# Sliding-window attention of a fused encoder layer: from half chunks to whole chunks

## The chip, the cores and the metric

The kernel runs on one core of one Trainium2 chip, as one launch. The metric is the time of that launch on the device in microseconds, as the median of several runs; lower is better.

## The reference, cut to what matters

The program computes one layer of a streaming encoder in float32: 1024 prompt tokens and 64 sample tokens, model width 1024. The part that the change touches is sliding-window attention (SWA). Tokens come in chunks of 64: 16 chunks of the prompt and one of the sample, 17 in all. A chunk's 64 queries look at 192 keys (its own chunk and the two before it; the first two chunks of the prompt have 64 and 128 keys). There are 16 query heads of width 64 in two groups, and each group shares one key and value head.

```python
s = einsum('bnqhgd,bnkhd->bnhgqk', q, k) * 64 ** -0.5 + bias
m = maximum(max(s, axis=-1), sink)
e = exp(s - m)
p = e / (sum(e, axis=-1) + exp(sink - m))
out = einsum('bnhgqk,bnkhd->bnqhgd', p, v)
```

While SWA runs, the kernel also computes two products that need nothing from it, to keep TensorE busy: the values of the cross-attention memory, and the first output projection of the retention branch:

```python
mv = rms_norm(mem, g_mem) @ w_mv
a = (rms_norm(ret_o) * silu(ret_g)) @ w_ret_out
```

## The kernel before, in words

**Stages.** The kernel first projects the inputs (`project_phase`), with the large products done by Strassen's scheme (`strassen`, lines 208 to 211). Then comes the stage of the change (`mix_phase`, which calls `swa`), and after it the merge of the branches, cross-attention and the feed-forward network. A float32 product is made of three matmuls on rounded parts: `mm3` (lines 152 to 154) multiplies high by high, high by low and low by high. So each operand is first split in two: ScalarE rounds it (line 125) and VectorE subtracts (line 126).

**One half of a chunk.** 64 queries times 2 heads fill 128 partitions, so a chunk's 16 heads are 8 units, and a half (`hf`) is 4 of them. `scores` multiplies queries by keys into PSUM (line 1188; these matmuls use 64 of the 128 rows of the array), VectorE adds the bias into the tile `t` (line 1195, or 1201 for the two short chunks) and finds the minimum of each row (line 1198 or 1203). `softmax` has ScalarE take four exponentials with their sums (line 1214), VectorE invert the sums (line 1216) and GpSimd scale (line 1217). `turn` transposes the weights on TensorE with an identity matrix (line 1242 for the first 128 keys, line 1248 for the last 64); ScalarE copies the first result to SBUF (line 1243, tile `pT`) and VectorE the second (line 1249, tile `rT`). Once per chunk, `values` transposes the new value columns (line 1149) and ScalarE copies them out (line 1153). `weigh` multiplies by the values (lines 1259 and 1264) for a whole chunk, and VectorE copies the result into `osb` (line 1271), which is stored every other chunk.

**The order.** The loop at line 1279 runs over 34 halves. In one step TensorE gets: `weigh` of the last chunk (every other step), `scores` of the half two steps ahead, `turn` of this half, and then a piece or two of the other products. `in_order` keeps TensorE's instructions in the order of the program; on the other engines a scheduler sets the order when the kernel is built, and each engine then works strictly through its list. `fill` hands out the pieces: 8 of the memory values before the first `turn`, 40 of the output projection over the 34 steps, and 8 more behind the last `weigh`. A piece is 12 matmuls for the projection (4 blocks of `mm3`), and 12 for the values (24 matmuls per block of 128 memory tokens).

**The other products.** `filler` makes the memory values of two heads: `us` are the split weights, line 1356 scales the result out of PSUM and frees its bank, and two stores follow on SyncE's queue. Then it multiplies by `w_ret_out`: units 0, 1 and 2 (each 128 output columns) are loaded and split together before the first product, the split of 1 and 2 behind the last of those scaled copies (line 1365); `m_major` then goes through the three units chunk of tokens by chunk of tokens. During the first eight pieces, `operands` also splits the retention output of the remaining tokens (tiles `ret`, lines 125 and 126), two per piece, 16 in all. Line 1377 multiplies a finished product by the gate.

**PSUM.** There are eight banks. Before `mix_phase`, the projections use three pairs of banks in turn (`psa`) and two single ones. `mix_phase` then takes, in this order, `pturn` (two banks, for line 1242 and line 1248), `pout` (a pair, for `weigh`), `pw` (a pair, for `scores`) and two single banks for the pieces. So `scores` stands on the third pair of `psa`.

Of the kernel before, what the change touches and what calls it, by code (L numbers as in the profile page):

```python
# [14 lines left out]
ALU = mybir.AluOpType  # L15
# [95 lines left out]
class Kernel:  # L111
# [999 lines left out]
    def swa(self, ctx, fill):  # L1111
        nc, tc, io = self.nc, self.tc, self.io
        if True:
# [27 lines left out]

            def values(los):
# [4 lines left out]
                pt = self.dense_psum()  # L1147
                for j, lo in enumerate(new):
                    self.last_mm = nc.tensor.transpose(pt[:n, j * P:(j + 1) * P], flat[5][:, 64 + lo:64 + lo + n], self.ident).ins
                at = vts[0][0]  # L1150
                for lo in new:
                    vtok[lo] = vts.pop(0)[1]
                nc.scalar.copy(at[:n, :len(new) * P], pt[:n, :len(new) * P])
# [3 lines left out]
            halves = [(c, hf) for c in range(17) for hf in range(2)]  # L1157
            live, outs, self.turn_copy = {}, {}, None
# [19 lines left out]

            def scores(c, hf):
                ks, j0, nk = keys(c)  # L1180
                if hf == 0 and c % 4 == 2 and c + 2 < 17:
# [3 lines left out]
                pss = pw.tile([P, 2, 512], F32, tag="s", name="pss")  # L1185
                for i in range(2):
                    for v in range(2):
                        self.last_mm = mm(pss[:, v, i * NKEY:i * NKEY + nk], qT[rows[v], 2 * hf + i, c % 4, :],  # L1188
                                          kT[rows[v], ks:ks + nk], start=True, stop=True).ins
                t = logits[hf]  # L1190
                ps = pss[:, :, :2 * NKEY].rearrange("p v (i n) -> p v i n", n=NKEY)
                bs = bias.rearrange("p (v h i) n -> p v h i n", v=2, h=2)[:, :, hf]
                nm = sw.tile([P, 2, 2], F32, tag="nm", name="nm")
                if nk == NKEY:
                    nc.vector.scalar_tensor_tensor(t[:, :, 1:wide_row - 1], pss[:, :, :2 * NKEY], -0.125,
                                                   bs.rearrange("p v i n -> p v (i n)"), ALU.mult, ALU.subtract)
                    both = t.rearrange("p v (i n) -> p v i n", i=2)
                    self.max_done = nc.vector.tensor_reduce(nm, both, AX.X, ALU.min).ins  # L1198
                else:
                    for i, x in enumerate(inner(t, nk)):  # L1200
                        nc.vector.scalar_tensor_tensor(x, ps[:, :, i, :nk], -0.125, bs[:, :, i, j0:], ALU.mult, ALU.subtract)
                    for i, x in enumerate(parts(t, nk)):
                        self.max_done = nc.vector.tensor_reduce(nm[:, :, i:i + 1], x.unsqueeze(2), AX.X, ALU.min).ins
                live[c, hf] = nm

            def softmax(c, hf):
# [17 lines left out]

            def turn(c, hf):
                ks, j0, nk = keys(c)
                wide = nk == NKEY
                if hf == 0:
                    values([ks + P, ks - 64, ks + 64, ks] if wide else [ks])
                    tail = [vtok[ks + P], vtok[ks - 64]] if wide else None  # L1230
                    live[c] = [vtok[ks + 64 * i if wide else ks] for i in range(2)], tail
                    tall = sw.tile([P, 4, 2, P], F32, tag="pT0", bufs=1, name="pT")
                    rest = sw.tile([P, 2, 2, P], F32, tag="pT1", bufs=1, name="rT") if wide else None
                    outs[c] = tall, rest
                tall, rest = outs[c]
                t = live.pop((c, hf))
                n = min(P, nk)
                pp = self.pt.tile([P, 512], F32, tag="pt0", name="pp")
                for j, (v, i) in enumerate(units):
                    a = 64 * i if wide else 0  # L1240
                    x = inner(t, nk)[i][:, v, a:a + n]
                    self.last_mm = nc.tensor.transpose(pp[:n, j * P:(j + 1) * P], x, self.ident).ins
                self.turn_copy = nc.scalar.copy(tall[:n, :, hf, :], pp[:n, :].rearrange("p (u q) -> p u q", u=4)).ins
                if wide:
                    pp = self.pt.tile([P, 512], F32, tag="pt1", name="pr")
                    for v in range(2):
                        x = t[:, v, 1 + P:1 + 2 * P]
                        self.last_mm = nc.tensor.transpose(pp[:, v * P:(v + 1) * P], x, self.ident).ins
                    nc.vector.tensor_copy(rest[:, :, hf, :], pp[:, :2 * P].rearrange("p (v q) -> p v q", v=2))

            def weigh(c):
# [9 lines left out]
                if rest is not None:  # L1261
                    for v in range(2):
                        for i in range(2):
                            self.last_mm = mm(po[rows[v], i, :2 * P], tail[i][rows[i], rows[v]], row(rest[rows[i], v]),
                                              start=False, stop=True).ins
                if c % 2 == 0:
                    outs["osb"] = sw.tile([P, KT, 2, 64], F32, tag="osb", bufs=2, name="osb")
                osb = outs["osb"]
                to = osb[:, :, c % 2, :].rearrange("p (h i e) q -> p h i e q", h=2, i=2)
                for i in range(2):  # L1270
                    nc.vector.tensor_copy(to[:, :, i], po[:, i, :2 * P].rearrange("p (h e q) -> p h e q", h=2, e=2))
                if c % 2 == 1 or c == 16:
# [4 lines left out]

            n = len(halves)
            for i in range(-2, n):
                if i > 0 and i % 2 == 0:  # L1280
                    self.in_order(lambda: weigh(i // 2 - 1))
                if i + 2 < n:
                    self.in_order(lambda: scores(*halves[i + 2]))
                if i >= 0:
                    self.in_order(lambda: turn(*halves[i]))
                if i + 2 < n:
                    softmax(*halves[i + 2])
                for pieces in next(fill):
                    self.in_order(lambda: next(pieces, None))
                if i == 8:  # L1290
                    with tc.issue_after(self.last_fetch):
                        keep()
            self.in_order(lambda: weigh(n // 2 - 1))
            for pieces in next(fill):
                self.in_order(lambda: next(pieces, None))

# [17 lines left out]
    def filler(self):  # L1314

        nc, tc, io = self.nc, self.tc, self.io
        if True:
# [24 lines left out]
            for h in range(2, H):  # L1342
# [5 lines left out]
                for t in range(2):  # L1348
# [6 lines left out]
                    o = ld()[:, :256]  # L1355
                    copied = nc.scalar.mul(o, ps[:, :256], self.mtok[:, t:t + 1]).ins
                    self.store(self.d_mv[h, :, t, :], o)
                    self.store(io["o_mv"][t * P:(t + 1) * P, h * 256:(h + 1) * 256], o)
                    yield

            def unit(m):
                raw = self.unit_raw(io["w_ret_out"][m], KT)
                if m not in (1, 2):
                    return self.unit_parts(raw, KT)
                with tc.issue_after(copied):
                    return self.unit_parts(raw, KT)

            units = [lambda m=m: unit(m) for m in range(KT)]
            for m, u, (c0, n) in self.m_major(units, CH, tail=1, lead=3):
                g = ld()  # L1370
# [651 lines left out]
```

## Time and profile before

| | us |
|---|---|
| median of three runs | 2193.73 |
| lowest and highest of them | 2190.91, 2196.80 |
| the profiled execution's own time | 2199.11 |
| its span, first to last instruction | 2197.1 |
| stage of the change: first `scores` | 804.2 |
| stage of the change: last `weigh` begins | 988.1 |

Times inside the profile count from the start of the span. PE is TensorE, DVE is VectorE, ACT is ScalarE, POOL is GpSimd and SP is SyncE. A row of the timeline gives start, duration, engine, line, operation, tiles, shape and count; in brackets stands how long the engine had been idle and what released it. PE is busy in 98% of the span, so what counts is the few microseconds in which it isn't, and the time that its own instructions take. A matmul's duration overlaps the next, so a cost on PE is read from starts. PEclk is the share of TensorE's clock that was granted.

### The profile page before, as it was taken

What the parts mean: (1) busy time and instruction counts of PE and PEld (TensorE: products, weight loads), DVE (VectorE), ACT (ScalarE), POOL (GpSimd) and SP (SyncE); (2) the same over time, 40 slices, a digit from 0 to 9 for tenths busy, and PEclk for the clock granted to TensorE, in tenths of its full rate; (3) what the DMA queues carried; (4) which work ended last, traced back from release to release, by engine and by line L of the source; (5) the groups of instructions that cost most, each with busy time, mean ns of one, the idle gap of its engine ahead of it and who ended that gap; (6) DMA issues with size and microseconds to landing.
All of it is one profiled execution on the core that took longest, in us unless ns stands there. A gap on an engine that the chain in (4) does not pass through costs nothing.

```text
span 2197.1 us, 41242 instructions
## 1 busy us (share of the span) xinstructions
PE 2154.6 (98%) x16388; PEld 2104.8 (96%) x16388; DVE 1574.0 (72%) x2569; ACT 875.0 (40%) x1826; POOL 616.9 (28%) x472
## 2 busy tenths in 40 slices
PE   9999999999999999999999999999999999999988
PEld 9999999999999997779999999999999999999987
DVE  7897878767678658766445555668877777779777
ACT  6434343436434356553233333333223222334333
POOL 0014535452264213220000000016655555431121
PEclk9999999999999999999999999999999999999999
DMA  4533434443454475427443121412432232466332
GB/s 172 185 113 113 145 115 158 131 133 108 142 181 158 146 252 185 133 73 226 131 156 114 40 69 55 139 60 95 142 122 96 93 130 80 147 245 221 112 106 92
DMA packets 160370, 291.84 MB, mean 133 GB/s; under 512 B 20946, under 2 KB 89490, under 8 KB 160050
## 3 DMA queue, kind: packets, MB, share of 16 engines
q1 hardware_dynamic: 150466, 263.41, 37.1%
q0 software_dynamic: 5104, 17.44, 2.2%
q10 hardware_dynamic: 4608, 8.36, 1.0%
q8 instruction: 129, 2.11, 0.4%
q14 instruction: 63, 0.52, 0.1%
HBM read 197.99 MB, written 91.95 MB: 132 GB/s over the span
## 4 chain that ended last, share of the span: by engine, by line
PE 79%; DVE 8%; DMA 6%; ACT 3%; issue 2%; POOL 2%; SPq 0%; DVEq 0%; ACTq 0%; POOLq 0%
PE pq L208 16%; PE pq L211 15%; PE pq L209 15%; PE pd L152 7%; PE pd L154 7%; PE pd L153 7%; DVE wq L126 1%; ACT e L1214 1%; DMA raw<-w_down 1%; PE pss L1188 1%; DVE stage L659 1%; DMA d_qkv<-stage 1%; DMA xg<-xT 1%; PE pk L894 1%; PE pout L1259 1%
## 5 line engine op out<-in xcount | busy, mean ns | idle before, releaser
L126 DVE TENSOR_TENSOR wq<-raw,wq 128x512 fp32r<-128x512 f32 (+1 forms) x498 | 454.5, 918 | 165.3 <-ACT wq L125 163.5
L125 ACT CAST wq<-raw 128x512 fp32r<-128x512 f32 (+1 forms) x498 | 299.5, 612 | 558.3 <-PE pq L211 186.4
L208 PE MATMUL pq<-T,wq 128*128 128x272 f32 x1800 | 496.1, 293 | 11.5 <-ACT wq L125 10.7
L209 PE MATMUL pq<-T,wq 128*128 128x272 f32 x1800 | 490.7, 289 | 0.0
L208 PE MATMUL pq<-B,wq 128*128 128x272 f32 x1550 | 424.3, 292 | 1.4 <-DVE stage L659 1.3
L209 PE MATMUL pq<-B,wq 128*128 128x272 f32 x1550 | 419.8, 288 | 0.0
L211 PE MATMUL pq<-T,wq 128*128 128x272 f32 x1800 | 374.2, 289 | 2.1 <-DVE wq L126 2.1
L186 POOL TENSOR_TENSOR raw<-raw 128x512 f32<-128x512 f32 (+1 forms) x49 | 69.1, 1411 | 1034.6 <-DVE rs_r L316 476.6
L208 PEld LDWEIGHTS pq<-T,wq 128*128 128x128 f32 x1800 | 341.4, 190 | 14.1 <-ACT wq L125 11.3
L209 PEld LDWEIGHTS pq<-T,wq 128*128 128x128 f32 x1800 | 344.8, 192 | 0.0
L211 PE MATMUL pq<-B,wq 128*128 128x272 f32 x1550 | 320.4, 287 | 0.0
L209 PEld LDWEIGHTS pq<-B,wq 128*128 128x128 f32 x1550 | 294.4, 190 | 0.0
L208 PEld LDWEIGHTS pq<-B,wq 128*128 128x128 f32 x1550 | 291.5, 188 | 2.7 <-ACT mraw L568 1.5
L211 PEld LDWEIGHTS pq<-T,wq 128*128 128x128 f32 x1800 | 281.2, 189 | 2.5 <-DVE wq L126 2.3
L211 PEld LDWEIGHTS pq<-B,wq 128*128 128x128 f32 x1550 | 240.2, 188 | 0.0
L277 DVE TENSOR_TENSOR u<-pq,u 128x544 f32<-128x544 f32 x174 | 124.6, 718 | 67.2 <-PE pq L211 66.9
L659 DVE TENSOR_TENSOR stage<-pq,u 128x544 f32<-128x544 f32 x108 | 77.4, 717 | 32.5 <-PE pq L211 22.8
L189 POOL TENSOR_TENSOR raw<-raw 128x512 f32<-128x512 f32 (+1 forms) x49 | 68.0, 1387 | 83.1 <-DVE wq L126 78.9
L1217 POOL TENSOR_TENSOR e<-e,den 128x768 f32<-128x768 f32 (+2 forms) x38 | 49.2, 1299 | 127.4 <-DVE den L1216 114.7
L1214 ACT ACTIVATE e<-t,nm 128x193 f32<-128x193 f32 (+2 forms) x136 | 59.1, 436 | 49.2 <-DVE nm L1198 48.3
L152 PE MATMUL pd<-xc,wq 128*128 128x256 f32 (+1 forms) x256 | 74.6, 291 | 0.2 <-DVE qf L1490 0.2
L192 POOL TENSOR_TENSOR raw<-raw 128x512 f32<-128x512 f32 (+1 forms) x49 | 70.4, 1437 | 15.3 <-DVE wq L126 12.2
(408 smaller groups left out, 4707.4 us busy)
## 6 DMA issues: line engine op xcount, KB each, us to landing
hl<-d_op SPq DMA_DIRECT2D x38, 544.0 KB, 5.2
d_op<-stage SPq DMA_DIRECT2D x44, 272.0 KB, 2.2
d_op<-ht SPq DMA_DIRECT2D x44, 272.0 KB, 3.3
raw<-w_gate SPq DMA_DIRECT2D x22, 512.0 KB, 3.5
raw<-w_up SPq DMA_DIRECT2D x22, 512.0 KB, 4.9
raw<-w_down SPq DMA_DIRECT2D x16, 512.0 KB, 3.8
d_gate<-stage ACTq DMA_DIRECT2D x28, 272.0 KB, 2.5
d_qkv<-stage SPq DMA_DIRECT2D x24, 272.0 KB, 2.3
```

Source lines behind the costliest of these rows:

```text
L125: self.last_cast = self.nc.scalar.copy(hi, src).ins
L126: self.last_low = self.nc.vector.tensor_tensor(out=lo, in0=src, in1=hi.bitcast(F32), op=ALU.subtract).ins
L152: mm(ps, wh, xh, start=start, stop=False)
L153: mm(ps, wh, xl, start=False, stop=False)
L154: self.last_mm = mm(ps, wl, xh, start=False, stop=stop).ins
L192: self.last_sum = tt(out=a12, in0=a12, in1=a11, op=sub).ins
L208: mm(ps[:, c, :HC], w[:, 0, ks], x[:, 0, cs], start=start, stop=False)
L209: mm(ps[:, c, :HC], w[:, 0, ks], x[:, 1, cs], start=False, stop=False)
L211: self.last_mm = mm(ps[:, c, :HC], w[:, 1, ks], x[:, 0, c * HC:(c + 1) * HC], start=False, stop=stop).ins
L277: add = lambda out, a, b: nc.vector.tensor_tensor(out=out, in0=a, in1=b, op=ALU.add)
L659: nc.vector.tensor_tensor(out=o, in0=ps, in1=sb, op=ALU.add)
L1214: self.exp_done = nc.scalar.activation(parts(e, nk)[i][:, v], parts(t, nk)[i][:, v], AF.Exp, scale=-1.0, bias=nm[:, v, i:i + 1], accum_out ...
```

## The change

1. **Whole chunks.** The loop runs over 17 chunks. TensorE's order in one step becomes: `weigh` of the last chunk, `scores` of both halves of the next chunk, a piece or two, `turn` of both halves of this chunk, a piece or two. `turn` copies both halves' first 128 keys at once (line 1244, 1024 elements per partition, where line 1243 had 512) and both rests at once (line 1252).
2. **Logits ahead of minima and copies.** VectorE adds the bias for both halves first, then finds the minima of both. The copies of the result into `osb` move from `weigh` into `gather` and stand behind the minima.
3. **Exponentials.** Those of the first half no longer stand behind the copy of the last `turn`; those of the second half still do.
4. **Values turned beside the rest.** `values` no longer takes a bank of the pieces: it writes into the second bank of the pair that `turn` uses for the rests, and its copy is line 1151.
5. **Pools swapped.** `pturn` is gone. `pw` comes first and has two pairs of banks, one per half, used by `scores` and then by `turn`; `pout` comes after it.
6. **First output weights.** Units 0 and 1 of `w_ret_out` are loaded together, unit 2 when it is first needed; units 1 and 2 are split at first use, behind the last copy of a `turn` on ScalarE.

```diff
-            self.pt, self.po, self.pw = (ctx.enter_context(self.tc.tile_pool(name=n, bufs=1, reuse_waits="tile", space=PSUM))
-                                         for n in ("pturn", "pout", "pw"))
+            self.pw, self.po = (ctx.enter_context(self.tc.tile_pool(name=n, bufs=1, reuse_waits="tile", space=PSUM))
+                                for n in ("pw", "pout"))
...
-                yield [pieces] * 4
-                yield [pieces] * 4
+                yield [pieces] * 8
...
+            area = lambda hf, name: pw.tile([P, 2, 512], F32, tag=f"s{hf}", name=name)
...
+                        self.max_done = nc.vector.scalar_tensor_tensor(
+                            t[:, :, 1:wide_row - 1], pss[:, :, :2 * NKEY], -0.125,
+                            bs.rearrange("p v i n -> p v (i n)"), ALU.mult, ALU.subtract).ins
+                        mins.append((nm, t.rearrange("p v (i n) -> p v i n", i=2)))
...
+                for nm, x in mins:
+                    with tc.issue_after(self.max_done):
+                        self.max_done = nc.vector.tensor_reduce(nm, x, AX.X, ALU.min).ins
...
-                with tc.issue_after(self.turn_copy) if self.turn_copy is not None else nullcontext():
+                with tc.issue_after(self.turn_copy) if hf and self.turn_copy is not None else nullcontext():
...
+                pr = area(1, "pr")
+                values([ks + P, ks - 64, ks + 64, ks] if wide else [ks], pr[:, 1, :])
...
+                self.turn_copy = nc.scalar.copy(tall[:n].rearrange("p u h q -> p h u q"),
+                                                pp[:n].rearrange("p h (u q) -> p h u q", u=4)).ins
...
+            for c in range(-1, 17):
+                if c > 0:
+                    self.in_order(lambda: weigh(c - 1))
+                if c < 16:
+                    self.in_order(lambda: scores(c + 1))
+                if c > 0:
+                    gather(c - 1)
+                if c < 16:
+                    softmax(c + 1, 0)
+                filled()
+                if c >= 0:
+                    self.in_order(lambda: turn(c))
+                if c < 16:
+                    softmax(c + 1, 1)
+                if c >= 0:
+                    filled()
...
+            raws = [self.unit_raw(io["w_ret_out"][m], KT) for m in range(2)]
+            done = {}
+
             def unit(m):
...
+                if m not in done:
+                    raw = raws[m] if m < 2 else self.unit_raw(io["w_ret_out"][m], KT)
+                    with tc.issue_after(self.turn_copy) if m in (1, 2) else nullcontext():
+                        done[m] = self.unit_parts(raw, KT)
+                return done[m]
```

The order in which instructions stand on an engine is fixed in the built program. Three places show what moved. The first is ScalarE around the memory values, before the change: `e` are the exponentials, `pd` the bank that line 1356 reads and frees, `wq` a split weight.

```order
L1214 ACT_TABLE_LOAD
L1214 ACTIVATE e_9694,den_9695<-t_9680,nm_9689 128x65 x4
L1356 ACTIVATE swin2_9521<-pd_9711,mtok_72 128x256
L125 CAST wq_9789<-raw_9641 128x512
L125 CAST wq_9792<-raw_9643 128x512
L125 CAST wq_9795<-raw_9643 128x512
L1356 ACTIVATE swin0_9424<-pd_9739,mtok_72 128x256
L1214 ACTIVATE e_9777,den_9778<-t_9681,nm_9772 128x65 x4
```

The same place after the change; line 1372 is what line 1356 was.

```order
L1215 ACT_TABLE_LOAD
L1215 ACTIVATE e_9701,den_9702<-t_9677,nm_9686 128x65 x4
L1215 ACTIVATE e_9842,den_9843<-t_9678,nm_9694 128x65 x4
L1372 ACTIVATE swin2_9521<-pd_9718,mtok_72 128x256
L125 CAST wq_9777<-raw_9641 128x512
L125 CAST wq_9780<-raw_9643 128x512
L125 CAST wq_9783<-raw_9643 128x512
L1372 ACTIVATE swin0_9424<-pd_9746,mtok_72 128x256
```

Both halves' exponentials now stand ahead of the first scaled copy and of three weight casts. The second place is ScalarE around chunk 0's `turn`, before the change: `pT` is the copy of line 1243, and `swin4<-pd` of line 1153 the copy of the turned values, both read by `weigh`.

```order
L125 CAST wq_9893<-raw_9891 128x512
L125 CAST wq_9896<-raw_9891 128x512
L1153 COPY swin4_9672<-pd_9864 128x128
L1243 COPY pT_9867<-pp_9868 64x4x128
L125 CAST wq_9901<-raw_9899 128x512
L125 CAST wq_9904<-raw_9899 128x512
L1214 ACTIVATE e_9874,den_9875<-t_9680,nm_9859 128x129 x4
L125 CAST ret0_9489<-swin6_9430 128x384
L125 CAST ret1_9492<-swin6_9430 128x384
L1243 COPY pT_9867<-pp_9937 64x4x128
```

After the change, the copy of the turned values is line 1151.

```order
L1215 ACTIVATE e_9871,den_9872<-t_9677,nm_9856 128x129 x4
L125 CAST ret0_9489<-swin6_9430 128x384
L125 CAST ret1_9492<-swin6_9430 128x384
L1244 COPY pT_9913<-pp_9914 64x2x4x128
L1215 ACTIVATE e_9924,den_9925<-t_9678,nm_9864 128x129 x4
L125 CAST ret4_9526<-swin6_9430 128x384
L125 CAST ret5_9529<-swin6_9430 128x384
L125 CAST wq_9986<-raw_9882 128x512
L125 CAST wq_9989<-raw_9882 128x512
L1151 COPY swin4_9669<-pr_9910 128x128
```

The copy of the turned values moved from ahead of everything to behind the second half's exponentials, two operand casts and the two casts of unit 1. The third place is VectorE in one later chunk, before the change.

```order
L1195 SCALAR_TENSOR_TENSOR t_9680<-pss_10402,swin2_9521 128x2x384
L1249 COPY rT_10414<-pr_10421 128x2x128
L1198 TENSOR_REDUCE nm_10407<-t_9680 128x4
L1377 TENSOR_TENSOR swin0_9424<-pd_10376,swin0_9424 128x384
L1195 SCALAR_TENSOR_TENSOR t_9681<-pss_10447,swin2_9521 128x2x384
L1216 RECIPROCAL den_10426<-den_10426 128x4
L1249 COPY rT_10414<-pr_10461 128x2x128
L1198 TENSOR_REDUCE nm_10452<-t_9681 128x4
```

And after the change.

```order
L1194 SCALAR_TENSOR_TENSOR t_9677<-pss_10378,swin2_9521 128x2x384
L1194 SCALAR_TENSOR_TENSOR t_9678<-pss_10385,swin2_9521 128x2x384
L1205 TENSOR_REDUCE nm_10383<-t_9677 128x4
L1205 TENSOR_REDUCE nm_10390<-t_9678 128x4
L1279 COPY osb_10394<-pout_10368 128x2x2x64 x2
L1396 TENSOR_TENSOR swin0_9424<-pd_10351,swin0_9424 128x384
L1217 RECIPROCAL den_10398<-den_10398 128x4
L1252 COPY rT_10423<-pr_10419 128x2x2x128
```

Both additions of the bias now come first, then both minima, then the copies; the copy of the rests is one instruction.

More of the change, by code (lines that the diff above doesn't have):

```diff
@@ L1140, in swa, with values @@
             vtok = {}
-            def values(los):
+            def values(los, pt):
                 new = [lo for lo in los if lo not in vtok]
@@ L1177, in keys, with scores @@
                 return kc + j0, j0, NKEY - j0
-            def scores(c, hf):
+            def scores(c):
                 ks, j0, nk = keys(c)
-                if hf == 0 and c % 4 == 2 and c + 2 < 17:
+                if c % 4 == 2 and c + 2 < 17:
                     with tc.issue_after(self.last_fetch):
@@ L1184, in scores @@
                 qT = qTs[c // 4 % 2]
[L1185 to L1203, printed above, removed]
@@ L1223, in softmax, with turn @@
                 live[c, hf] = e
-            def turn(c, hf):
+            def turn(c):
                 ks, j0, nk = keys(c)
                 wide = nk == NKEY
[L1228 to L1236, printed above, removed]
-                n = min(P, nk)
[L1238 to L1243, printed above, removed]
-                if wide:
[L1245 to L1249, printed above, removed]
@@ new lines, in turn @@
+                pr = area(1, "pr")
+                values([ks + P, ks - 64, ks + 64, ks] if wide else [ks], pr[:, 1, :])
+                tail = [vtok[ks + P], vtok[ks - 64]] if wide else None
+                live[c] = [vtok[ks + 64 * i if wide else ks] for i in range(2)], tail
+                tall = sw.tile([P, 4, 2, P], F32, tag="pT0", bufs=1, name="pT")
+                rest = sw.tile([P, 2, 2, P], F32, tag="pT1", bufs=1, name="rT") if wide else None
+                outs[c] = tall, rest
@@ new lines, in turn @@
+                es = [live.pop((c, hf)) for hf in range(2)]
+                n = min(P, nk)
+                pp = area(0, "pp")
+                for hf, e in enumerate(es):
+                    for j, (v, i) in enumerate(units):
+                        a = 64 * i if wide else 0
+                        x = inner(e, nk)[i][:, v, a:a + n]
+                        self.last_mm = nc.tensor.transpose(pp[:n, hf, j * P:(j + 1) * P], x, self.ident).ins
+                self.turn_copy = nc.scalar.copy(tall[:n].rearrange("p u h q -> p h u q"),
+                                                pp[:n].rearrange("p h (u q) -> p h u q", u=4)).ins
@@ L1251, in weigh @@
+                if wide:
+                    pr = pr[:, 0, :]
+                    for hf, e in enumerate(es):
+                        for v in range(2):
+                            j = 2 * hf + v
+                            self.last_mm = nc.tensor.transpose(pr[:, j * P:(j + 1) * P], e[:, v, 1 + P:1 + 2 * P], self.ident).ins
+                    nc.vector.tensor_copy(rest.rearrange("p v h q -> p h v q"), pr.rearrange("p (h v q) -> p h v q", h=2, v=2))
             def weigh(c):
@@ L1265, in weigh, with gather @@
                                               start=False, stop=True).ins
+                live["po"] = po
+            def gather(c):
+                po = live.pop("po")
                 if c % 2 == 0:
@@ L1276, in weigh, with filled @@
                                osb.rearrange("p m a q -> p m (a q)")[:, :, :n])
[L1278 to L1287, printed above, removed]
+            def filled():
                 for pieces in next(fill):
                     self.in_order(lambda: next(pieces, None))
-                if i == 8:
+            for c in range(-1, 17):
[14 more added lines that the diff above has]
+                    filled()
+                if c == 4:
                     with tc.issue_after(self.last_fetch):
                         keep()
-            self.in_order(lambda: weigh(n // 2 - 1))
-            for pieces in next(fill):
-                self.in_order(lambda: next(pieces, None))
+            self.in_order(lambda: weigh(16))
+            gather(16)
+            filled()
     def load_queries(self, qTs, c):
@@ L1355, in filler @@
                     o = ld()[:, :256]
-                    copied = nc.scalar.mul(o, ps[:, :256], self.mtok[:, t:t + 1]).ins
+                    nc.scalar.mul(o, ps[:, :256], self.mtok[:, t:t + 1])
                     self.store(self.d_mv[h, :, t, :], o)
@@ L1359, in filler @@
                     yield
+            raws = [self.unit_raw(io["w_ret_out"][m], KT) for m in range(2)]
+            done = {}
             def unit(m):
[L1362 to L1369, printed above, removed]
+                if m not in done:
[3 more added lines that the diff above has]
+                return done[m]
+            for m, u, (c0, n) in self.m_major([lambda m=m: m for m in range(KT)], CH, tail=1, lead=3):
+                u = unit(m)
                 g = ld()
```

22 lines of the change are left out of this document (18 added, 4 removed).

## The prediction

> **What bounds the kernel now.** I read the page first, then the windows around the stage of the change, TensorE's waits in it, and the timelines of PE, ACT and DVE. A change of under 0.3%, 6.6 us, can't be told from none here. The page says that PE is the bound:
>
> ```profile
> span 2197.1 us, 41242 instructions
> PE 2154.6 (98%) x16388; PEld 2104.8 (96%) x16388; DVE 1574.0 (72%) x2569; ACT 875.0 (40%) x1826; POOL 616.9 (28%) x472
> ```
>
> The windows (columns: length, then busy time and instructions of PE, PEld, DVE, ACT and POOL, then PEclk, DMA share and GB/s) say where in the stage it isn't:
>
> ```profile
> 801.50:804.20 2.70, 0.01 (x1) 0.01 (x1) 2.67 (x6) 1.69 (x4) 1.15 (x3) 1.00 0.66 146
> 804.20:811.00 6.80, 6.80 (x35) 6.68 (x36) 2.51 (x9) 4.12 (x12) 1.40 (x4) 0.50 0.64 245
> 861.00:900.00 39.00, 37.81 (x300) 30.04 (x296) 29.96 (x51) 22.91 (x82) 11.94 (x9) 1.00 0.45 140
> 900.00:976.00 76.00, 76.00 (x578) 62.40 (x571) 53.23 (x96) 42.64 (x157) 22.04 (x15) 1.00 0.27 83
> ```
>
> From 900 to 976 PE is never idle: there the change can only save PE's own time. Before that it is idle in places, and once its clock is halved for 6.8 us, right after 2.70 us of idleness. TensorE's waits from 798 to 992 (total, times, longest) are short:
>
> ```profile
> PE pout L1259 <- ACT pT L1243: 4.5, 6, 2.1
> PE pss L1188 <- DVE stage L659: 2.7, 1, 2.7
> PE pp L1242 <- POOL e L1217: 1.3, 1, 1.3
> PE pss L1188 <- DVE t L1195: 1.0, 2, 0.7
> PE pr L1248 <- DVE rT L1249: 0.3, 1, 0.3
> ```
>
> So 9.8 us of waits and some half clock are all there is to win as stalls, 0.6% at most. The rows of PE that carry the sums:
>
> ```profile
> 804.20 1.12 PE L1188 MATMUL pss<-swin,swin 64*128 64x64 f32 x8 [2.70 <-DVE stage L659]
> ...
> 813.72 0.66 PE L1188 MATMUL pss<-swin,swin 64*128 64x64 f32 x8
> 820.26 0.71 PE L1188 MATMUL pss<-swin,swin 64*128 64x128 f32 x8
> 820.91 0.33 PE L1149 MATMUL pd<-ident,swin 128*128 128x128 f32 x1
> ...
> 829.19 1.08 PE L1259 MATMUL pout<-pT,swin 64*64 64x256 f32 x8 [2.13 <-ACT pT L1243]
> ...
> 860.23 1.08 PE L1259 MATMUL pout<-pT,swin 128*64 128x256 f32 x8 [0.54 <-ACT pT L1243]
> 861.24 0.66 PE L1264 MATMUL pout<-rT,swin 64*64 64x256 f32 x8
> 861.83 0.92 PE L1188 MATMUL pss<-swin,swin 64*128 64x192 f32 x8
> 862.68 0.33 PE L1149 MATMUL pd<-ident,swin 128*128 128x128 f32 x1
> ...
> 869.45 1.08 PE L1259 MATMUL pout<-pT,swin 128*64 128x256 f32 x8
> ```
>
> **Term 1, the swapped pools.** The first `scores` waits 2.70 us for line 659, the last product of the projections: `pw` sits on that product's banks. After the change `pw` sits on the two pairs before it, read long since, so `scores` starts at 804.20 - 2.70 = 801.5. The chunk's 16 scores and the 48 value matmuls of the first head then follow. One set of 8 scores and 48 matmuls takes 813.72 - 804.20 = 9.5 us at half clock and 820.26 - 813.72 = 6.5 at full, so half clock cost 3.0 in one 6.8 us stretch. At full clock PE is through at about 801.5 + 0.6 + 6.5 = 808.6. What is late next is ACT:
>
> ```profile
> 806.12 1.28 ACT L1214 ACT_TABLE_LOAD   x1
> 807.41 0.35 ACT L1214 ACTIVATE e<-t,nm 128x65 f32<-128x65 f32 x1
> ...
> 808.67 0.19 ACT L1214 ACTIVATION_READ_ACCUMULATOR e<-t,nm 128x1 f32 x1
> 810.77 0.47 ACT L1356 ACTIVATE swin<-pd,mtok 128x256 f32<-128x256 f32 x1 [1.91 <-PE pd L154]
> 811.73 2.06 ACT L125 CAST wq<-raw 128x512 fp32r<-128x512 f32 x3 [0.49 <-PE pd L154]
> ```
>
> Four exponentials take 807.41 to 808.86, 1.45 us. Nothing before them moves, so they still start at 807.4; now eight stand ahead of the scaled copy: 807.4 + 2.9 = 810.3, and the copy frees the bank at 810.8. The second head's products need that bank, so PE waits 808.6 to 810.8, a new hole of 2.2 us. With 5.9 us for the 48 products and 0.4 for the weight casts that follow the copy, the values end at 817.1, against 820.2: gain 3.1.
>
> **Term 2, the first `weigh`.** Before, it waits 2.13 us, to 829.19. These ACT rows are its chain:
>
> ```profile
> 822.58 0.26 ACT L1153 COPY swin<-pd 128x128 f32<-128x128 f32 x1
> ...
> 825.14 1.15 ACT L125 CAST wq<-raw 128x512 fp32r<-128x512 f32 x2 [1.83 <-DMA raw<-w_ret_out]
> 826.19 0.40 ACT L1214 ACTIVATE e<-t,nm 128x129 f32<-128x129 f32 x1
> ...
> 827.75 0.91 ACT L125 CAST ret<-swin 128x384 fp32r<-128x384 f32 x2
> 828.56 0.57 ACT L1243 COPY pT<-pp 64x512 f32<-64x512 f32 x1
> ```
>
> The casts of unit 2 wait for its load, and hold up the copy behind them. That load now comes later and out of the way. But the order puts the copy of the turned values (line 1151), which `weigh` reads, behind the second half's exponentials and four casts. From the end of the next `scores` (817.1 + 1.3 = 818.4) the chain is: four additions of 256 elements 1.6 (0.4 each by the 768-element row below), the first half's minima 0.8, four exponentials 1.55 (826.19 to 827.75), two operand casts 0.91, the doubled turn copy 1.0 (between 0.57 for one half and 1.16 for two; nearer two), four exponentials 1.55, two operand casts 0.91, two weight casts 1.15, the copy 0.26: 9.7 us, so 828.1. PE itself needs 12 + 12 matmuls and the transposes, 5.5 us, and is ready at 823.9: a hole of 4.2. The first `weigh` starts at 828.1 against 829.19. Of the 3.1 us, 1.1 are left. Bounds: if the scheduler's order costs nothing, 823.9 (gain 5.3); if the weight casts in this chain wait for their load once more, by the 1.83 us of the row above, 829.9 (loss 0.7).
>
> **Term 3, chunks 1 to 4.** Here two to four operand casts per step stand ahead of the turn copy, and the copy waits for a longer chain than before: additions of both halves, the first minima, exponentials.
>
> ```profile
> L1198 DVE TENSOR_REDUCE nm<-t 128x4 f32<-128x772 f32 x30 | 28.3, 945 | 0.0
> L1195 DVE SCALAR_TENSOR_TENSOR t<-pss,swin 128x768 f32<-128x768 f32 x30 | 28.3, 944 | 4.1 <-PE pss L1188 4.0
> ...
> L1243 ACT COPY pT<-pp 128x512 f32<-128x512 f32 x32 | 18.6, 581 | 8.1 <-PE pp L1242 8.1
> ```
>
> and, in the chain of waits, eight exponentials in a row:
>
> ```profile
> 974.00 1.88 ACT e L1214 x8
> ```
>
> From the end of `scores`: 0.2 (the first addition ran beside the second half's scores) + 0.9 + 0.9 + 1.9 + 1.0 = 4.9, and a few 0.1 of hand-over; PE's own work until `weigh` is 12 matmuls, 15 transposes and 12 matmuls, 2.2 + 1.7 + 2.0 = 5.9. With two casts it is 5.9 against 5.9, with four (each followed by a VectorE subtraction ahead of the next addition) 8, and unit 2's split, now in line behind the second half's exponentials and two casts, holds the product of chunk 2 by about 2.4. I take holes of 0.5, 2.4, 1.8 and 0.5 us for chunks 1 to 4, 5.2 in all, where the stalls of before in the same stretch are 9.8 less 2.7, 2.13, 1.3 and 1.2 (the part after 869), 2.5: loss 2.7. Bounds: no hole, gain 2.5; all holes doubled, loss 8. By `weigh` of chunk 4 the change is 1.6 us behind.
>
> **Term 4, twelve plain chunks.** Per chunk one change from half-height to full-height weights and back goes. By the rows, 8 scores until the first transpose take 820.91 - 820.26 = 0.65 us at 128 columns and 862.68 - 861.83 = 0.85 at 192; so 64 columns cost 0.2, the scores 0.6, and the change to transposes 0.25. I take 0.2 per chunk after what the new joints cost: 12 x 0.2 = 2.4. The waits left in this stretch go (POOL 1.3, the turn copies after 869 about 1.2, 0.2 others): 2.7, since the chain of 4.9 fits into 5.9. Where pieces have 320 columns the cover is thinner, about 0.4 us; if that goes, each chunk pays (rival C). VectorE's moved copies and the gather hide beside the pieces: it is busy 53 of 76 us.
>
> **The sum.** +1.6 - 2.4 - 2.7 = -3.5. Against that stands the clock. A row for another hole:
>
> ```profile
> 1968.00:1971.50 3.50, 3.50 (x18) 3.50 (x18) 2.69 (x4) 0.42 (x2) 1.33 (x1) 0.52 0.13 19
> ```
>
> The hole of 2.70 at 801.5 was followed by half clock, the one of 2.13 at 829 was not; the new one of 4.2 is the longest of the stage. I take one stretch of 3.4 us at half clock, 1.5 us. Sum: -2.0.
>
> [...]
>
> The profiled execution took 2199.11, 2.0 outside its span, and lies 5.4 over the median of 2193.73. Its own time would become 2197.1; the median 2191.7.
>
> **The rivals.** A, the forecast: PE stays the bound, the early part is paced by ACT, and the gain is a few us: 2188 to 2196, likeliest 2191.7; chance 0.65.
>
> B, the stalls go and none comes: terms 1 (3.1), 2 and 3 without holes (2.2 + 2.5), 4 (5.1) give -13 at best, -9 if half of the early holes stay: 2181 to 2185. For it: the waits removed are real. Against: the two orders on ACT. Chance 0.17.
>
> C, slower: the single turn copy becomes the pace. It stands behind the first half's exponentials, so the chain of 4.9 us plus hand-overs grows with every cast that lands between. If it exceeds PE's work by 0.8 us in the twelve plain chunks, these cost 9.6 rather than nothing: +7.6 on the forecast, 2199 to 2201. It decides from 5.9 us of chain on (5.3 beside 320-column pieces). Against: 76 us without a single idle PE cycle and ACT busy 43 of them. Chance 0.08.
>
> D, the swap does nothing for the start, since the exponentials stand at 807.4 whatever PE does, and the early holes eat the rest: within 1 us of before, 2193.7. Chance 0.10.
>
> **How the numbers follow.** Faster by over 0.3% is below 2187.1: B's 0.17 and 0.06 of A. Slower is above 2200.3: 0.05 of C. The rest, 0.72, is no difference. The range takes in A and D whole and parts of B and C: 2185.5 to 2198.
>
> **What would show it.** Right: the first `scores` at 801.5; a PE hole of about 2 us before the second head's products, released by line 1372; one of about 4 before the first `weigh`, released by line 1151, at about 828; chunks of 9.0 us from 900 on, where 9.2 stood. Wrong: no PE wait on ACT between 805 and 860 (B), or a PE wait on line 1244 in most of the later chunks (C).

## The result, and the profile after

The changed kernel takes 2226.18 us (median of four runs, 2224.82 to 2232.89), the kernel before 2193.34 (four runs, three of which are in the table above). The ratio is 1.0153, with a 95% interval of 1.0138 to 1.0167: slower by 1.5%, some 33 us, where the forecast was 2 us faster and the range ended at 2198.

The page of the changed kernel: the matmuls are the same in number, and the span is 26.6 us longer.

```profile
span 2223.7 us, 41210 instructions
...
PE 2160.6 (97%) x16388; PEld 2114.0 (95%) x16388; DVE 1570.5 (71%) x2554; ACT 872.9 (39%) x1809; POOL 617.6 (28%) x472
```

The windows of the changed kernel, over the same stretches as before (columns as in the prediction):

```profile
861.00:900.00 39.00, 30.02 (x220) 24.79 (x220) 23.16 (x38) 18.68 (x65) 9.77 (x7) 0.95 0.31 98
900.00:976.00 76.00, 66.43 (x471) 55.21 (x471) 41.79 (x71) 34.91 (x123) 19.88 (x14) 0.91 0.28 86
```

Where PE was never idle before, from 900 to 976, it is now idle for 9.6 us, and its mean clock is 0.91. It got through 471 matmuls there, where it did 578. TensorE's waits in the stage (total, times, longest) name the place:

```profile
PE pr L1251 <- ACT swin L1151: 25.5, 11, 2.7
PE pout L1262 <- ACT swin L1151: 3.0, 1, 3.0
PE pd L152 <- ACT swin L1372: 2.8, 1, 2.8
PE pd L154 <- DVE wq L126: 1.4, 1, 1.4
PE pd L152 <- ACT wq L125: 0.4, 1, 0.4
```

Line 1251 transposes the rests, line 1151 copies the turned values out. In 11 of the 15 chunks that have rests, the transposes wait for that copy, 2.3 us on average. They have no use for the values. Both write the tile `pr`, the values into its second bank and the rests into its first, and the program makes a write into the tile wait for the reader of what was written there before. One such chunk in the timeline of the changed kernel:

```profile
943.18 0.62 ACT L125 CAST wq<-raw 128x512 fp32r<-128x512 f32 x1 [4.45 <-PE pd L154]
...
943.70 0.45 ACT L1215 ACTIVATE e<-t,nm 128x193 f32<-128x193 f32 x1
...
943.85 0.27 PE L1147 MATMUL pr<-ident,swin 128*128 128x128 f32 x1
...
945.03 0.44 ACT L1215 ACTIVATE e<-t,nm 128x193 f32<-128x193 f32 x1
...
945.47 0.99 ACT L1244 COPY pT<-pp 128x1024 f32<-128x1024 f32 x1
...
946.36 0.26 ACT L1151 COPY swin<-pr 128x128 f32<-128x128 f32 x1
...
946.67 0.65 PE L1251 MATMUL pr<-ident,e 128*128 128x128 f32 x4 [2.55 <-ACT swin L1151]
```

The values are turned at 943.85. Their copy takes 0.26 us, but on ScalarE it stands behind four exponentials of the next chunk and behind the doubled turn copy, so it begins 2.5 us after them. From 944.12, the end of line 1147, TensorE stands still in front of the rests. In chunks 4 to 15 the holes have two lengths: 1.9 us in four chunks, and 2.55 to 2.70 in five, where a weight cast of 0.62 us (the first row) stood ahead of the exponentials as well. With the hole the clock often drops, too: in all five chunks with that cast, in one of the four without. Two windows of the changed kernel, the hole and what came 0.8 us behind it (columns as in the prediction):

```profile
943.96:946.67 2.71, 0.16 (x2) 0.00 (x0) 1.92 (x6) 2.66 (x10) 0.62 (x1) 1.00 0.32 98
...
947.50:950.90 3.40, 3.40 (x14) 2.96 (x12) 0.81 (x2) 1.57 (x8) 1.40 (x2) 0.50 0.87 256
```

The other four chunks are a control inside the same profile. In three of them two pieces stand ahead of `turn`, not one, so that the exponentials are through by then (the fourth is the last chunk, which has no next exponentials), and the copy of the values stands ahead of the turn copy:

```profile
958.45 0.27 PE L1147 MATMUL pr<-ident,swin 128*128 128x128 f32 x1
...
958.56 0.82 PE L1243 MATMUL pp<-ident,e 128*128 128x128 f32 x6
958.76 0.27 ACT L1151 COPY swin<-pr 128x128 f32<-128x128 f32 x1 [0.65 <-PE pr L1147]
...
959.22 0.60 PE L1251 MATMUL pr<-ident,e 128*128 128x128 f32 x4
959.42 1.02 ACT L1244 COPY pT<-pp 128x1024 f32<-128x1024 f32 x1 [0.39 <-PE pp L1243]
```

Here the copy is done at 959.0, while TensorE is still at the first transposes, and line 1251 follows without a wait.

**The account of the stage.** A window from where TensorE is free for the first `scores` to the last `weigh` holds the same work in every kernel, 1305 matmuls (1306 where one more touches an edge). Of the changed kernel:

```profile
799.48:1018.78 219.30, 186.03 (x1305) 158.99 (x1304) 130.66 (x223) 105.06 (x354) 51.63 (x42) 0.92 0.38 120
```

and of the kernel before, from 801.5, where TensorE was free:

```profile
801.50:988.11 186.61, 176.69 (x1305) 146.62 (x1305) 132.04 (x237) 107.25 (x370) 50.96 (x42) 0.98 0.45 141
```

The stage is 32.7 us longer, as much as the medians differ (32.8). Idle time is the length less PE's busy time: 219.3 - 186.0 = 33.3 after, 186.6 - 176.7 = 9.9 before, 23.4 more. The rest, 9.3 us more of busy time, holds two things: more half clock (ten stretches of 3.41 us after, one of 6.8 before), and PE's own work. The first experiment gives an estimate of each. (Outside the stage the profiled execution was 6.1 us faster than the one of before, 2.0 ahead of it and 4.1 behind it, in code that is the same; so its span grew by only 26.6.)

### The profile page after: what moved, and what is told of

Its sections match the earlier page's. It is cut to its first block, busy times and chain, and to the rows that moved or that the text cites. A ratio compares the mean times of both kernels' runs of the same rounds, so it can differ in the third digit from the quotient of the medians.

```text
span 2223.7 us, 41210 instructions
## 1 busy us (share of the span) xinstructions
PE 2160.6 (97%) x16388; PEld 2114.0 (95%) x16388; DVE 1570.5 (71%) x2554; ACT 872.9 (39%) x1809; POOL 617.6 (28%) x472
## 4 chain that ended last, share of the span: by engine, by line
PE 51%; DVE 2%; DMA 1%; ACT 0%; issue 0%; POOL 0%; SPq 0%; DVEq 0%; ACTq 0%; POOLq 0%
PE pq L208 10%; PE pq L211 10%; PE pq L209 10%; PE pd L152 6%; PE pd L154 6%; PE pd L153 6%; DMA raw<-w_down 1%; DMA ld<-d_swa 0%; PE cpo L152 0%; PE css L154 0%; PE cpo L153 0%; PE css L152 0%; PE cpo L154 0%; PE css L153 0%; PE cpt L1531 0%; DVE wq L126 0%
## 5 line engine op out<-in xcount | busy, mean ns | idle before, releaser
L126 DVE TENSOR_TENSOR wq<-raw,wq 128x512 fp32r<-128x512 f32 (+1 forms) x498 | 448.0, 906 | 160.0 <-ACT wq L125 158.2
L208 PEld LDWEIGHTS pq<-T,wq 128*128 128x128 f32 x1800 | 340.2, 189 | 12.3 <-ACT wq L125 10.1
```

The source lines that it names most:

```text
L126: self.last_low = self.nc.vector.tensor_tensor(out=lo, in0=src, in1=hi.bitcast(F32), op=ALU.subtract).ins
L208: mm(ps[:, c, :HC], w[:, 0, ks], x[:, 0, cs], start=start, stop=False)
```

## The experiments

Two theories. **S, the shared tile:** the loss is the wait of the rests for the copy of the values, and the half clock that its holes bring. **T, the turn copy** (rival C of the prediction): ScalarE's chain of exponentials and one doubled turn copy is too late for whole chunks; if the rests didn't wait for it, `weigh` would. (The expectations call experiments 1 to 4 e1, e2, e3 and e5, the kernels of experiment 5 e6 to e9, and those of experiment 6 e10 and e11.)

**1. The values in a bank of the pieces again.**

```diff
-                values([ks + P, ks - 64, ks + 64, ks] if wide else [ks], pr[:, 1, :])
+                values([ks + P, ks - 64, ks + 64, ks] if wide else [ks], self.dense_psum())
```

> The changed kernel with one thing undone: the turned values go into a bank of the pieces again (as before the change), not into the second bank of the tile that takes the rests. Theory S (shared tile): in the changed kernel the transposes of the rests (line 1251) wait 25.5 us in 11 of 15 chunks for the copy of the values (line 1151), because both write one tile, and these holes bring some eight stretches of half clock, 3.4 us each, with at most 1.7 us lost in each. Without the shared tile both go: 2226 - 25.5 - about 11 = 2190 us (2185 to 2197), no wait of line 1251, at most two half-clock stretches between 800 and 1000. Theory T (turn copy, rival C of the prediction): ScalarE's chain of exponentials and the doubled turn copy is late by itself; the hole moves from line 1251 to weigh (line 1262 on line 1244) and the time stays over 2210.

Measured: 2193.74 us against 2194.45 for the kernel before on the same chip, ratio 1.000 (0.9986 to 1.0014). One line takes the whole loss away. TensorE's waits in the stage of this kernel, and the stage's window:

```profile
PE pd L152 <- DVE swin L1396: 3.4, 4, 2.1
PE pout L1262 <- ACT pT L1244: 2.8, 4, 1.2
PE pd L154 <- DVE wq L126: 1.8, 1, 1.8
PE pd L152 <- ACT swin L1372: 1.3, 1, 1.3
PE pr L1251 <- DVE t L1194: 0.3, 1, 0.3
...
```

```profile
800.58:984.68 184.10, 173.74 (x1305) 148.48 (x1305) 129.96 (x221) 101.65 (x351) 50.56 (x41) 0.98 0.45 143
```

The rests no longer wait for ScalarE. `weigh` does wait for the turn copy, as T has it, but 2.8 us in four chunks, not in all. S holds, and T has a small part of what it claimed. Two stretches of half clock are left in the stage; each costs at most 1.7 us, half its 3.41 us at a clock of 0.50, so PE's own work is about 173.7 - 3.4 = 170.3 us. Before it was about 176.7 - 3.4 = 173.3. So whole chunks save some 3.0 us of TensorE's work, and in the changed kernel, if its own work is that of this one, half clock cost 186.0 - 170.3 = 15.7 us. The loss of 32.7 is then 23.4 of idleness, plus 15.7 - 3.4 = 12.3 of half clock, less 3.0 of work saved.

**2. The values in unused columns of `pout`.** They are turned behind the rests, into the tile that `weigh` will write.

```diff
-                values([ks + P, ks - 64, ks + 64, ks] if wide else [ks], pr[:, 1, :])
...
+                po = self.po.tile([P, 2, 512], F32, name="pout")
+                values([ks + P, ks - 64, ks + 64, ks] if wide else [ks], po)
```

> The changed kernel with the values turned into the unused columns of the tile that weigh writes, behind the transposes of the rests; weigh has to wait for the copy of the values in any case, so the tile adds no wait. No bank of the pieces is taken. Theory S: as e1 or a little better, since no piece waits for the bank: 2188 us (2183 to 2195). Theory T: over 2210, with the wait at weigh.

Measured: 2206.91 us, ratio 1.0058 (1.0042 to 1.0073). 19 us less than the changed kernel, but between the two figures: neither theory's came, and S's range was missed by 12 us. The waits of this kernel, and a chunk of its timeline:

```profile
PE pout L1264 <- ACT swin L1153: 11.3, 10, 1.5
PE pout L1147 <- DVE osb L1281: 3.9, 6, 1.7
...
```

```profile
950.41 0.60 PE L1250 MATMUL pr<-ident,e 128*128 128x128 f32 x4
...
952.03 0.99 ACT L1243 COPY pT<-pp 128x1024 f32<-128x1024 f32 x1
...
952.92 0.46 ACT L1217 ACTIVATE e<-t,nm 128x193 f32<-128x193 f32 x1
...
954.26 0.44 ACT L1217 ACTIVATE e<-t,nm 128x193 f32<-128x193 f32 x1
...
954.70 0.24 ACT L1153 COPY swin<-pout 128x128 f32<-128x128 f32 x1
...
954.99 1.08 PE L1264 MATMUL pout<-pT,swin 128*64 128x256 f32 x8 [1.49 <-ACT swin L1153]
```

The rests (line 1250 here) go at 950.41, 1.6 us ahead of the turn copy and without any wait, with ScalarE just as late as in the changed kernel. So it isn't lateness on ScalarE that stopped the rests, but the tile: that speaks for S. My own step was wrong: "`weigh` waits for the copy in any case" took the copy to be early. It had moved behind the second half's exponentials too, and 1.8 us of them (952.92 to 954.70) now stand between the turn copy and `weigh`. (The second of the waits shown is a price of this kernel alone: the values need the tile of `weigh` before VectorE has copied the last result out of it.)

**3. The copy of the values ahead of the turn copy, the tile still shared.**

```diff
-                nc.scalar.copy(at[:n, :len(new) * P], pt[:n, :len(new) * P])
+                self.val_copy = nc.scalar.copy(at[:n, :len(new) * P], pt[:n, :len(new) * P]).ins
...
+                with tc.issue_after(self.val_copy):
+                    self.turn_copy = nc.scalar.copy(tall[:n].rearrange("p u h q -> p h u q"),
...
```

> The changed kernel, tile still shared, but on ScalarE the copy of the values always stands ahead of the turn copy (only the order of these two is fixed). Theory S: the rests no longer wait through the turn copy's 0.99 us, but still through the exponentials that stand ahead; 11 holes shrink by 1.0 us each, 11 us, and three or four half-clock stretches go, 5 us: 2210 us (2205 to 2217). Theory T: the turn copy comes 0.26 us later in 11 chunks, so the same or slower: 2226 to 2229.

Measured: 2208.06 us, ratio 1.0067 (1.0046 to 1.0088), inside S's interval and far from T's. The wait (line 1252 here) and the stage:

```profile
PE pr L1252 <- ACT swin L1151: 17.4, 11, 3.4
...
```

```profile
807.18:1006.45 199.27, 175.26 (x1306) 149.23 (x1305) 128.46 (x223) 103.29 (x354) 52.56 (x42) 0.97 0.42 132
```

The same 11 chunks wait, 8.1 us less in all, yet the stage is 219.3 - 199.3 = 20.0 us shorter (the medians differ by 18.1). Idle time accounts for 33.3 - 24.0 = 9.3, and busy time for 10.8: in the plain chunks most holes now last 1.0 to 1.7 us, and the ten stretches of half clock in the stage became the length of three. So about half of what the shorter holes gave came with the clock. That the total fell inside S's interval is partly luck: 11 us of waits and 5 of half clock were expected to go, and 8.1 and some 10.8 went.

**4. The kernel before with its pools swapped, and nothing else.** In the order `pw`, `pturn`, `pout`.

```diff
-            self.pt, self.po, self.pw = (...
-                                         for n in ("pturn", "pout", "pw"))
+            self.pw, self.pt, self.po = (...
+                                         for n in ("pw", "pturn", "pout"))
```

> The kernel before with the order of its three PSUM pools changed only (pw first, then pturn, pout). Term 1 of the prediction: the first scores no longer wait 2.70 us, the half clock after that goes (3.0 us), and ScalarE's four exponentials at 807.4 set a hole of about half a us: 3 to 5.5 us faster, 2188 to 2191 against 2193.7. Rival D: the exponentials stand where they stood, so under 1 us: 2193 to 2194.

Measured: 2192.57 us, ratio 0.9996 (0.9982 to 1.001): no difference that can be told. Two of its waits:

```profile
PE pout L1259 <- ACT pT L1243: 5.3, 4, 4.1
PE pd L152 <- ACT swin L1356: 1.4, 1, 1.4
...
```

The first `scores` no longer wait. But TensorE then reaches the first `weigh` sooner than ScalarE does, and what was a hole of 2.13 us there is one of 4.1 with 6.8 us of half clock. The stall moved from one place to the next: the 3 to 5.5 us of Term 1 didn't come, and the time is that of the prediction's rival D, for this part alone.

**5. Four kernels that try to keep what whole chunks save.** In the first, the values of the next chunk are turned at the end of a step, ahead of `weigh`, into the shared tile; those of chunk 0 stay where they were.

```diff
-                values([ks + P, ks - 64, ks + 64, ks] if wide else [ks], pr[:, 1, :])
+                live["pr"] = pr
+                if c == 0:
+                    values(need(0), pr[:, 1, :])
...
+                if 0 <= c < 16:
+                    self.in_order(lambda: values(need(c + 1), live["pr"][:, 1, :]))
```

> The changed kernel, but the values of the next chunk are turned at the end of a step, just ahead of weigh, into the second bank of the tile of the rests. The tile stays shared, yet nothing writes it soon after: the next writer is scores, some 2 us later. Theory S (shared tile): no wait of the rests, as in e1; and since no bank of the pieces is taken, e1's 3.4 us of waits for line 1396 and one of its two half-clock stretches (at most 1.7 us) go too: 2188 to 2191 us. If the pieces' bank cost e1 nothing that counts, the same as e1: 2192 to 2195. If scores now waits for the copy of the values behind the second half's exponentials, about 1 us in each of 15 chunks: 2205 and more.

> e6 with the first output weights loaded and split as before the change (all three units ahead of the first product). Term 2 and 3 of the prediction: the split on ScalarE and VectorE behind the turn copy (1.8 us of wait of line 154 for line 126 in e1, with a half-clock stretch at 827.5, 1.7 us at most) goes, 2 to 3 us faster than e6. Rival: the casts ahead of chunk 0's turn copy hold the first weigh as they did before (2.13 us), and the time is that of e6 within 1.5 us.

> e6, with the second half's four exponentials of chunk 0 put behind the first scaled copy of the memory values (line 1372 in the changed kernel) on ScalarE. Term 1 of the prediction: the hole ahead of the second head's products (2.77 us in the changed kernel, 1.28 in e1) shrinks by the 1.5 us of four exponentials, and the stretch of half clock behind it goes: 1.5 to 3 us faster than e6. Rival: those exponentials, 1.5 us later, hold chunk 0's turn instead: the same as e6 within 1 us.

> e1 with the first output weights as before the change. If change 6 costs what line 154's wait for line 126 shows (1.8 us and up to 1.7 us of half clock): 2190 to 2192. If the casts ahead of the first turn copy cost as much: 2193 to 2196.

Measured: 2196.31 (ratio 1.0007, 0.9994 to 1.0019), 2195.22 (0.9998, 0.9984 to 1.0012), 2195.76 (1.000, 0.9985 to 1.0015) and 2194.43 (0.9994, 0.9981 to 1.0008). All four are the kernel before, as far as this can be measured. (One of the second kernel's twelve executions took 8511 us; without it the median is 2194.49.) For the first none of the three times that had been named came, and the other three came out at the times of their rivals, not at the gains. The waits of the first of them:

```profile
PE pd L152 <- ACT swin L1380: 3.2, 1, 3.2
PE pout L1268 <- ACT swin L1151: 3.0, 1, 3.0
PE pr L1147 <- DVE rT L1258: 2.8, 4, 1.1
PE pss L1188 <- ACT swin L1151: 1.2, 1, 1.2
...
```

With the tile shared as in the changed kernel, but with its other writer 2 us away, the rests don't wait: S once more. The third row is the same rule from the other side: now the values wait for VectorE's copy of the rests, out of the other bank of that tile. From the `weigh` of chunk 5 to the last the stage takes 106.3 us, as in experiment 1 (106.2; the kernel before 108.0), but chunk 0's copy is late again, so the two long holes at the start are back (lines 1380 and 1151). The early part is a set of waits on ScalarE of which taking one away lengthens another: undoing the weights' split made the hole ahead of the first `weigh` 5.2 us in the second kernel, and moving the exponentials in the third left 0.6 and 0.9 us of the first hole's 3.2 and the stage 1.7 us shorter, less than its total can show.

**6. Both starts mended.** In the first kernel of experiment 5, chunk 0's values go into a bank of the pieces (the edit is shown against that kernel); in the second one here the second half's exponentials of chunk 0 stand behind the first scaled copy as well.

```diff
                 if c == 0:
-                    values(need(0), pr[:, 1, :])
+                    values(need(0), self.dense_psum())
```

> e6, but chunk 0's values are turned into a bank of the pieces as in e1, ahead of its turn. In e1 the first weigh came 21.1 us after the first scores, in e6 27.2, where it waited 3.0 us for that copy; from chunk 5 on both need 106.2 to 106.3 us. If that copy is what holds the first weigh, 3 us of wait and one stretch of half clock (1.7 us at most) go: 2191 to 2193 us. If the turn copy of chunk 0 is next in line, no more than 1 us: 2195 to 2196.

> e10 and e8 together: chunk 0's values in a bank of the pieces, and the second half's exponentials of chunk 0 behind the first scaled copy. If both early holes go, the stage takes about 181 us where the kernel before took 186.6 from where TensorE was free: 2188 to 2190 us, faster than the kernel before by about 0.2%. If one hole only moves to the next wait of the early part: 2191 to 2195, no difference.

Measured: 2191.22 (ratio 0.9991, 0.998 to 1.0002) and 2191.88 (0.999, 0.9979 to 1.0001), the kernel before at 2194.18. The stage of the second:

```profile
799.95:982.85 182.90, 172.14 (x1305) 147.30 (x1304) 131.31 (x223) 102.90 (x354) 51.57 (x42) 0.99 0.45 144
```

182.9 us where the kernel before needed 186.6, with one stretch of half clock and 10.8 us of idleness. The first kernel did what was expected of it, as the wait of the first `weigh` is gone. The second didn't bring the stage to 181 us: the hole of 3.2 us ahead of the second head's products shrank to 1.3, but two new ones of 0.9 and 0.3 us came behind it. It is the shortest stage of all, and the medians agree, but 0.1% can't be told from none: the intervals end just over 1. So there is a version without the loss that may be 2 to 3 us faster than the kernel before; that it beats the kernel before isn't shown.

## Why the prediction was wrong

**Term 1, the start: the mechanism right, the size off.** The first `scores` start without a wait, and there is a hole ahead of the second head's products, released by line 1372, as forecast. In the rows of the changed kernel:

```profile
799.48 1.11 PE L1188 MATMUL pss<-swin,swin 64*128 64x64 f32 x16
...
809.30 0.39 PE L152 MATMUL pd<-wq,ms 128*128 128x256 f32 x1 [2.77 <-ACT swin L1372]
```

The hole is 2.77 us, 2.2 forecast. Behind it came 3.41 us of half clock, from 811.0, which I had charged to the other hole alone. The `scores` of chunk 1 start 817.13 - 799.48 = 17.7 us after the first, against 820.26 - 801.5 = 18.8: a gain of 1.1, not 3.1.

**Term 2, the first `weigh`: right in the main.** Its hole, released by line 1151, was 3.0 us (4.2 forecast), and `weigh` starts 826.68 - 799.48 = 27.2 us into the stage, against 27.7 before: a gain of 0.5, with 1.1 forecast. Here the prediction followed line 1151 into its place behind the exponentials, and it stopped there.

**Terms 3 and 4, the chunks: the step that failed.** Term 4 says that the waits of the plain chunks go, "since the chain of 4.9 fits into 5.9", and Term 3 works out its holes the same way. The 5.9 us were PE's work up to `weigh`, the reader of the turn copy. The chain has an earlier due date: the transposes of the rests, right behind the first transposes. Up to there PE has only one piece (in three chunks two) and nine transposes. The piece of the chunk shown begins here, as `scores` end:

```profile
941.11 0.41 PE L152 MATMUL pd<-ret,wq 128*128 128x320 f32 x1
```

To the end of line 1147, at 944.1, that is 3.0 us, where a chain of 4.9 and the 0.26 of the copy of the values make 5.2 (in the event the rests began 946.67 - 941.11 = 5.6 us after). What was said to be covered by 1.0 us lacked 2.2; the holes were 1.9 to 2.7, the longer ones with a cast in the chain. The chain was priced about right; the list of those who wait for it was not complete. The change itself says that the values are turned beside the rest, in its tile, and the prediction costed the copy of the values only where the values are read, not where the tile is written next. (One reading in that chain is wrong, though its price is right: the row `ACT e L1214 x8` of 1.88 us holds four exponentials and the four reads of their sums, not eight exponentials. Four is what stands ahead of the turn copy.)

**The parts of the stage.** The lengths in us, from where TensorE is free for the first `scores` to the last `weigh`. The forecast is the kernel before with the prediction's gains and losses; its 1.5 us for the clock are left out.

| part | before | forecast | after | experiment 1 |
|---|---|---|---|---|
| to the first `weigh` (Terms 1, 2) | 27.7 | 26.6 | 27.2 | 21.1 |
| to `weigh` of chunk 4 (Term 3) | 40.3 | 43.0 | 51.8 | 45.8 |
| to the last `weigh` (Term 4) | 118.7 | 113.6 | 140.3 | 117.2 |

The last part has no half clock before and in experiment 1, so PE's own work can be read there: 115.9 us of busy time before and 113.4 in experiment 1, a saving of 2.5 where Term 4 put 2.4. That it comes from fewer changes of weight height, as Term 4 has it, was not tried by itself. The idleness that Term 4 said would go did not, even without the shared tile: 2.8 us before, 3.8 in experiment 1, with other waits in the place of the old ones. So experiment 1 ends 2.5 us shorter in the stage, about what was forecast, by luck: the first part gained 5.5 us more than forecast, as its first hole is 1.3 us without half clock behind it and the copy of the values is early, so that the first `weigh` doesn't wait for it; and the other two lost 6.4 us of the forecast.

**The clock: wrong by a factor of ten.** One stretch of half clock, 1.5 us, was forecast, an estimate from the 6.8 us of the kernel before that cost 3.0; there were ten, of 3.41 us each, and they cost some 15.7 us, 12.3 more than before. With the holes wrong this had to be wrong; but it also means that the waits alone would have been 23 us, and that the clock made half as much again of them.

**The rivals.** C had the place (ScalarE's chain in the later chunks) and the direction, but named line 1244 as releaser and `weigh` as the one that waits, with a price of 0.8 us per chunk from 5.9 us of chain on. (Its 9.6 us are 7.6 more than the kernel before, not than the forecast.) In fact the point from which it decides lay at about 3, and the chain was past it from the start in each plain chunk with one piece ahead of `turn`. It had 0.08, and no sign on the prediction's list named a wait of line 1251. Without the shared tile the time would have been inside the range, though not by the prediction's sum: experiment 1 is the changed kernel with that one wait removed, and its median is 0.7 us below that of the kernel before, with 2.0 forecast and 3 us of interval either way.

## What to carry to other kernels

When a step moves into a tile that something else also uses, list the tile's next writer beside the value's reader: the program orders both, and the writer may be due much earlier. Then put the chain against the work that lies ahead of the first of them. A small copy costs what stands ahead of it in its engine's order: 0.26 us of ScalarE here held TensorE for 2.3 us in each of eleven chunks. And where TensorE is the bound, look for a second price of a hole in the clock: one of 2.55 us with 3.41 us at half clock behind it (1.7 us at most) cost about 4 here.

## What the runs showed of the hardware

The longer a hole, the more often the clock halved, and it did so at shorter lengths than the 2.70 us after which the prediction had seen it. All holes of TensorE of 0.9 us or more in the stage, over the twelve traces of this case, and how many had a stretch of half clock that began between their start and 2 us behind their end:

| hole, us | holes | with half clock |
|---|---|---|
| 0.9 to 1.7 | 39 | 1 |
| 1.7 to 2.2 | 17 | 6 |
| 2.2 to 5.3 | 20 | 19 |

Each stretch lasted 3.41 us or twice that, and in each trace all stretches of half clock begin a whole number of 3.413 us apart. The changed kernel's four holes of 2.55 us all brought half clock.

These starts give a grid, and the grid gives a second count. Cut into windows of 3.413 us along it, the stage has 647 windows at full clock in the twelve traces, and TensorE's idle share of each goes with what the next one is:

| TensorE idle in the window | windows | next one at half clock |
|---|---|---|
| under 45% | 612 | 0 |
| 45 to 55% | 11 | 3 |
| 55% and more | 24 | 24 |

So in this stage all 27 windows ahead of half clock had TensorE idle for 45% of their length or more, 1.5 us. How the grid cut a hole showed in the same way: the four holes of 2.55 us each took 67 to 75% of one window, and the one hole over 2.2 us that was missed, 2.63 us long, lay in two windows with idle shares of 36% and 42%.
